# One weight transfer at a time for both tiles of tokens in the feed-forward fronts, h in tiles of 512 by tile of tokens, and parting copies on ScalarE

## The chip, the cores and the metric

The kernel runs on one core of a Trainium2 chip. The metric is the device time of one execution in microseconds (us), median of several runs. A profile is one execution taken by the hardware profiler. Its engines are PE (TensorE, matmul; PEld is its weight load), DVE (VectorE), ACT (ScalarE), POOL (GpSimd), and SP (SyncE, which issues most DMAs).

## The reference, cut to what matters

A decoder trunk of two layers on 256 tokens of width 1024. Each layer is a feed-forward, a mixer and a second feed-forward, each followed by a layer norm:

```python
D_MODEL = 1024; SEQ = 256; DEPTH = 2; D_FF = 2816

def _swiglu(x, w1, w3, w2):
    return (jax.nn.silu(x @ w1) * (x @ w3)) @ w2
...
    for l in range(DEPTH):
        h = _swiglu(x, ffn_w1[l, 0], ffn_w3[l, 0], ffn_w2[l, 0])
        x = _layernorm(ALPHA * x + 0.5 * h, ln_g[l, 0], ln_b[l, 0])
        h = _mixer(...)                       # gated unit, differential attention, merge
        x = _layernorm(ALPHA * x + h, ln_g[l, 1], ln_b[l, 1])
        h = _swiglu(x, ffn_w1[l, 1], ffn_w3[l, 1], ffn_w2[l, 1])
        x = _layernorm(ALPHA * x + 0.5 * h, ln_g[l, 2], ln_b[l, 2])
```

All of it is float32. The change touches the four feed-forwards only.

## The kernel before, in words

**Products in three parts.** Each float32 number is split into a high part (a cast on ACT, `whi`, `hhi`) and the rest (a subtraction on DVE, `wlo`, `hlo`), and each product is three matmuls: high by high, high by low, low by high. Weights come from DRAM through `fetch`, one 1 MB transfer per chunk on SP's queue into one of four `raw` buffers; `stream` splits a chunk into two pieces of 128x1024, by casts and subtractions of width `sub`.

**The front of a feed-forward** (`ffn`) makes h = silu(x W1) * (x W3). Of its 22 column tiles of 128, 20 come in five blocks of 512 columns. Block 0 has a form of its own. Blocks 1 to 4 go through `gemm_b2`: for the first tile of 128 tokens it streams the four chunks of the block (two halves of the contraction `c`, by the two matrices `m`) and multiplies; then it goes over the same pieces again for the second tile of tokens. After each tile, `done` takes the silu of one bank on ACT (L723) and the product with the other on DVE (L724).

**Turning h.** The result has tokens on partitions, and the next matrix needs them on the free axis. So each tile of 128x512 is parted into its 16-bit halves (`parted`, two POOL copies, L199), turned by a DMA transpose that SP issues (`moved`, L203), and joined again (`joined`, POOL copies, L208); then it is split into `h_hi` and `h_lo` in pairs of 128x256 (L743, L745), in tiles that hold both tiles of tokens. These steps are a generator, `turned`, run `beside` the matmuls: it yields how many beats of matmul work to let pass before its next step, 13.3 or 10.3 between parting and transposing.

**The order of work.** TensorE's order is that of the program. On the other engines a scheduler orders by priority, and `behind(ins)` puts an instruction after another one on its engine's queue. The transpose is put behind the newest weight load:

```python
        yield first
        with behind(loaded[0]):
            moved(out, via)
```

**After the front**, two more column tiles come through `gemm_a2`, and `gemm_seven` multiplies by W2: for a square part of the problem by seven products of sums of blocks (L361, each 12 matmuls), each followed by as many ordinary matmuls (L376), then the remaining rows. It fetches two weight blocks into `spare` buffers, which hold x until `gemm_a2` is through with it, adds them on DVE (`plus`, L345), and later adds further blocks to them by accumulating DMAs from POOL's software queue (`gather`, L340):

```python
        product(bx, sums[2], pieces(gather(r2, w22)), False, False)
        ln.fold(1, 1, bx, ALU.subtract, False)
        between()
        product(bx, a22, pieces(gather(r1, w21)), False, True)
```

`fold` (L573, DVE) takes a product out of its bank, which the next product overwrites. Two rows of the norm (`bc`, L540) are loaded by the same software queue in that stage.

Of the kernel before, what the change touches and what calls it, by code (L numbers as in the profile page):

```python
# [54 lines left out]
def trunk(ctx, tc, x, xT, w13a, w13b, w2, wb, wqk, wu, wg, wgr, wbr, wbrr, wo, gateb, gatebr, sgug, sgub, sguwT, sgubias, lam, diffg,  # L55
# [18 lines left out]
    def name(s):  # L74
        serial[0] += 1
        return f"{s}_{serial[0]}"
# [75 lines left out]
    def fetch(src, width=CH, raw=None):  # L152

        step()
        if raw is None:
            raw = raw_pool.tile([P, CH], F32, tag="raw", name=name("raw"))
        for g in gate:
            g[0] -= 1
        while len(gate) > 1 and gate[1][0] < 0:
            gate.pop(0)  # L160
        with behind(gate[0][1] if gate and gate[0][0] < 0 else None):
            loaded[0] = nc.sync.dma_start(raw[:, :width], src).ins
        return raw

    def stream(src, width=CH, sub=HC, lent=(), after=(None, None), pool=()):
# [24 lines left out]
    def planes(v):  # L190
        return v.bitcast(U16).rearrange("p (w c) -> p w c", w=2)

    def numbers(v):
        return v.bitcast(U16).rearrange("p (c w) -> p w c", w=2)

    def parted(src, out):

        for w in range(2):
            G.tensor_copy(out=planes(out)[:, w], in_=numbers(src)[:, w])  # L199

    def moved(src, out):

# [4 lines left out]
        for w in range(2):  # L207
            eng.tensor_copy(out=numbers(out)[:, w], in_=planes(src)[:, w])  # L208

    def transposed(src, out, via, lead, first, second, eng, to=None):  # L210

        if lead:
            yield lead
        with behind(behind_norm[0] if lead else None):
            parted(src, out)
# [85 lines left out]
    def gemm_b(src, kts, xh, xl, done, tail=4, last=()):  # L303
# [13 lines left out]
        for t in range(NT):  # L317
            for ps, o, n in blocks[t]:
                for k, piece in held:
                    rows_b(ps, t, k, piece, xh, xl, kts, o, n)  # L320
                done(t, ps[:, :n], o, n)

    def gemm_seven(src, xh, xl, sums, spare, ln, done):


# [11 lines left out]
        def gather(raw, more):  # L337
            step()
            for o in range(0, CH, HC):
                G.dma_start(raw[:, o : o + HC], more[:, o : o + HC], accum_op=ALU.add)  # L340
            return raw

        def plus(raw, more):
            for o in range(0, CH, HC):
                V.tensor_tensor(out=raw[:, o : o + HC], in0=raw[:, o : o + HC], in1=more[:, o : o + HC], op=ALU.add)  # L345
            return raw

        def pieces(raw):
            out = []
            for o in range(0, CH, HC):  # L350
                hi = hi_pool.tile([P, HC], F32R, tag="hi", name=name("whi"))
                lo = lo_pool.tile([P, HC], F32R, tag="lo", name=name("wlo"))
                split(hi, lo, raw[:, o : o + HC])
                out.append((hi, lo))
            return out

        def product(ps, x, w, start, stop):
            for k in range(4):
                hi, lo = (v[:, k % 2 * 512 : k % 2 * 512 + 512] for v in w[k // 2])
                for n, (y, o) in enumerate(((hi, 0), (lo, 0), (hi, 1))):  # L360
                    PE.matmul(ps, x[o](k), y, start=start and k == n == 0, stop=stop and k == 3 and n == 2,  # L361
                              skip_group_check=True)
                beat(0.25)

        def rest(c):
            for k in range(8, FT, 4):
                nk = min(4, FT - k)
# [3 lines left out]
        def rows(t, c, k0, piece, o=0, n=512):  # L371
            for j in range(2):
                k = k0 + j
                hi, lo = (w[:, j * 512 + o : j * 512 + o + n] for w in piece)
                for m, (y, x) in enumerate(((hi, xh), (lo, xh), (hi, xl))):
                    PE.matmul(q[c][t][:, :n] if o == 0 else more[:, :n], x(k)[:, t * P : (t + 1) * P], y,  # L376
                              start=k == 8 and m == 0 and (c, t) != (1, 0), stop=k == FT - 1 and m == 2, skip_group_check=True)
            beat(n / 1024)

        def block(t, k0):  # L380
            return tuple(lambda k, f=f: f(k0 + k)[:, t * P : (t + 1) * P] for f in (xh, xl))

        a11, a12, a22 = block(0, 0), block(0, 4), block(1, 4)
        first = rest(0)
# [324 lines left out]

    def ffn(l, f, i, norm, last=False):  # L710
        xh, xl = parts(both)
        h_hi = [act.tile([P, 512], F32R, tag="slot", name=name("hhi")) for _ in range(FT // 2)]
        h_lo = [act.tile([P, 512], F32R, tag="slot", name=name("hlo")) for _ in range(FT // 2)]
        hh, hl = view(h_hi), view(h_lo)

        def front(n, wait):

            def done(t, ps):
                pool, tag = ((act, "val"), (res, "bc"))[n % 2]
                p = pool.tile([P, D], F32, tag=tag, name=name("planes"), bufs=2).rearrange("p (w c) -> p w c", w=2)  # L720
                s = p[:, 1]
                with behind(norm.xhi[1, 0] if norm and (n, t) == (0, 0) else None):
                    silu[0] = A.activation(s, ps[0], AF.Silu).ins  # L723
                added[0] = V.tensor_tensor(out=s, in0=s, in1=ps[1], op=ALU.mult).ins  # L724
                beside(turned(n, t, s, p, wait[t]), 0)
                if norm is None and (n, t) == (1, 0):
                    beside(setup(s[:, :1]), 0)
            return done

        def turned(n, t, s, p, wait):  # L730
            lead = 3.5 if n == 0 and norm else 0
            to = slots("held", 2)[0] if n < 2 else p[:, 0]
            yield from transposed(s, p[:, 0], p[:, 1], lead, wait - lead, 0.6, G, to)
            x = to.rearrange("p (k t) -> p k t", k=4)
            yield 0.6
            if n < 2:
                held[n, t] = to
            for j in range(2) if (n, t) != (0, 1) else ():
                k = (n * 4 if n < NB - 1 else FT - 4) // 2 + j
                hi, lo = (v[k].rearrange("p (k t) -> p k t", k=2)[:, :, t * P : (t + 1) * P] for v in (h_hi, h_lo))  # L740
                f = x[:, 2 * j : 2 * j + 2]
                with behind(silu[0]):
                    A.activation(hi, f, AF.Copy)  # L743
                with behind(added[0]):
                    V.tensor_tensor(out=lo, in0=f, in1=hi.bitcast(F32), op=ALU.subtract)  # L745
            if (n, t) == (1, 1):
                yield 1
                yield from sums_of_h()
# [3 lines left out]
        def sums_of_h():  # L752

            h11, h21, h12, h22 = (held[v] for v in ((0, 0), (0, 1), (1, 0), (1, 1)))
            made = [[[v[j].rearrange("p (k t) -> p k t", k=2)[:, :, P:] for j in range(2)] for v in (h_hi, h_lo)]]
            made += [[slots("sum", 2, F32R) for _ in range(2)] for _ in range(2)]
            made.append([[tmp.tile([P, 512], F32R, tag="side", name=name("sum"), bufs=4)] for _ in range(2)])
            sums[:] = [tuple(lambda k, v=v: hh_(v, k) for v in (h_hi, h_lo))]
            sums.extend(tuple(lambda k, v=v: v[0][:, k * P : (k + 1) * P] for v in m) for m in made[1:])
            for n, (out, a, b, op) in ((0, (h22, h21, h22, ALU.subtract)), (2, (h21, h11, h21, ALU.subtract)),  # L760
                                       (1, (h11, h22, h11, ALU.subtract)), (3, (h12, h12, h11, ALU.add))):
                V.tensor_tensor(out=out, in0=a, in1=b, op=op)
                w = 512 // len(made[n][0])
                for j, (hi, lo) in enumerate(zip(*made[n])):
                    f = out[:, j * w : (j + 1) * w]
                    split(hi, lo, f.rearrange("p (k t) -> p k t", k=2) if n == 0 else f)
                yield 1

        def hh_(v, k):
            return v[k // 2][:, k % 2 * T + P : k % 2 * T + T]  # L770

        for n in range(NB):
            srcs = [w13b[l, f, m * NB + n] for m in range(2)]
            if n == 0 and norm is None:
                gemm_first(srcs, front(n, (10.3, 10.3)))
            else:
                gemm_b2(srcs, xh, xl, front(n, (13.3, 10.3)), norm=norm if n == 0 else None)
        for j in range(FA, FT - 4, 2):
            for m, z in gemm_a2([w13a[l, f, j - FA + m] for m in range(2)], both, lambda m: t512("silu")):
                s = z[:, :T]  # L780
                silu[0] = A.activation(s, s, AF.Silu).ins
                V.tensor_tensor(out=s, in0=s, in1=z[:, T:], op=ALU.mult)
                split(hh(j + m), hl(j + m), s)
# [400 lines left out]
```

## Time and profile before

| what | value |
|---|---|
| median of 3 runs | 1199.59 us (1199.42 to 1200.43) |
| the profiled execution | 1198.81 us |
| its span | 1197.1 us |
| granted TensorE clock | 0.999 |
| DMA | 271.97 MB, 227 GB/s in the mean |

The span is the time from the first to the last instruction in the trace; the execution's own time is 1.7 us longer. A row of an engine's timeline has the start, the duration, the line, the operation and its tiles, and in brackets the idle time before it with what ended it. `waits` rows have the engine, what it waited for, and microseconds in total, times and longest. Rows of groups have busy time and mean duration in ns. Rows of windows have start and end, the length, and each engine's busy time with its count of instructions.

### The profile page before, as it was taken

To read this page: it belongs to the slowest core of one execution; us is meant where nothing else is said; L and a number is where in the kernel's file an instruction comes from. 1 tells how busy PE (TensorE), PEld (TensorE's weight loads), DVE (VectorE), ACT (ScalarE), POOL (GpSimd) and SP (SyncE) were. 2 spreads that over 40 slices of the span, in tenths; PEclk is the share of its full clock that TensorE was granted. 3 is DMA by queue.
4 is the path that set the end of the run, shared out by engine and by line. 5 is a ranking of instruction groups with operands and counts; after the bars stand their busy time and mean duration, and the time that the engine had idled before them with its cause. 6 is when DMAs were issued, how large, how long until landed. Compare 5 with 4: busy or idle time off the path is not lost.

```text
span 1197.1 us, 16880 instructions
## 1 busy us (share of the span) xinstructions
PE 1191.1 (100%) x5819; PEld 1002.1 (84%) x5819; DVE 958.4 (80%) x1632; ACT 745.9 (62%) x1424; POOL 363.0 (30%) x458
## 2 busy tenths in 40 slices
PE   9999999999999999999999999999999999999998
PEld 8888888888888888888888888888888888888887
DVE  6677989797689985769886769888966989777795
ACT  7466667668855664646665656666788556564670
POOL 1425201256421233251042351004564012325310
PEclk9999999999999999999999999999999999999999
DMA  9957966767865667689676679586666764775880
GB/s 350 332 163 238 273 263 211 260 198 233 243 218 169 211 220 220 193 245 265 238 241 205 196 241 275 223 287 232 214 203 200 254 193 150 269 230 178 265 253 36
DMA packets 126310, 271.97 MB, mean 227 GB/s; under 512 B 88672, under 2 KB 89744, under 8 KB 100112
## 3 DMA queue, kind: packets, MB, share of 16 engines
q1 hardware_dynamic: 119664, 248.80, 62.4%
q0 software_dynamic: 6128, 21.57, 7.4%
q8 instruction: 45, 0.74, 0.2%
q10 hardware_dynamic: 432, 0.52, 0.1%
q14 instruction: 41, 0.34, 0.1%
HBM read 244.91 MB, written 1.05 MB: 205 GB/s over the span
## 4 chain that ended last, share of the span: by engine, by line
PE 98%; DVE 1%; DMA 1%; ACT 0%; issue 0%; ACTq 0%
PE bank L262 53%; PE bank L274 15%; PE bank L376 9%; PE bank L281 8%; PE sbank L361 5%; PE sbank L376 3%; PE bank L480 2%; PE sbank L843 1%; PE bank L361 1%; PE sbank L899 1%; PE sbank L1017 1%; DMA bc<-in_lng 0%; PE sbank L897 0%; DMA xraw<-in_xT 0%; DVE wlo L186 0%; PE sbank L644 0%
## 5 line engine op out<-in xcount | busy, mean ns | idle before, releaser
L186 DVE TENSOR_TENSOR wlo<-raw,whi 128x512 fp32r<-128x512 f32 (+1 forms) x534 | 473.2, 927 | 52.4 <-ACT whi L184 36.0
L184 ACT ACTIVATE whi<-raw 128x512 fp32r<-128x512 f32 (+1 forms) x538 | 396.1, 782 | 165.7 <-PE bank L262 92.7
L262 PE MATMUL bank<-whi,x 128*128 128x512 f32 x1480 | 460.5, 390 | 0.0
L262 PEld LDWEIGHTS bank<-whi,x 128*128 128x128 f32 x1480 | 277.8, 188 | 57.7
L262 PE MATMUL bank<-wlo,x 128*128 128x512 f32 x740 | 288.0, 389 | 0.0
L199 POOL COPY planes<-planes 128x512 uint16<-128x512 uint16 x80 | 109.6, 1398 | 240.4 <-DVE planes L724 209.4
L262 PEld LDWEIGHTS bank<-wlo,x 128*128 128x128 f32 x740 | 138.9, 188 | 28.3
L274 PE MATMUL bank<-x,whi 128*128 128x512 f32 x640 | 153.3, 391 | 0.0
L274 PEld LDWEIGHTS bank<-x,whi 128*128 128x128 f32 x640 | 118.2, 188 | 23.8
L724 DVE TENSOR_TENSOR planes<-planes,bank 128x512 f32<-128x512 f32 x40 | 27.4, 684 | 75.3 <-issue 60.7
L723 ACT ACTIVATE planes<-bank 128x512 f32<-128x512 f32 x40 | 23.9, 596 | 99.4 <-PE bank L262 97.1
L281 PEld LDWEIGHTS bank<-x,wlo 128*128 128x128 f32 x640 | 81.4, 191 | 2.9
L281 PE MATMUL bank<-x,wlo 128*128 128x256 f32 x640 | 82.6, 283 | 0.0
L228 DVE TENSOR_TENSOR wlo<-raw,whi 128x1024 fp32r<-128x1024 f32 (+1 forms) x56 | 58.5, 1071 | 26.9 <-issue 18.4
L226 ACT ACTIVATE whi<-raw 128x1024 fp32r<-128x1024 f32 (+1 forms) x56 | 52.0, 937 | 42.5 <-DVE raw L345 18.8
L376 PE MATMUL bank<-whi,hhi 128*128 128x512 f32 (+1 forms) x182 | 68.2, 374 | 0.0
L376 PE MATMUL bank<-whi,hlo 128*128 128x512 f32 (+1 forms) x182 | 67.9, 373 | 0.0
L376 PE MATMUL bank<-wlo,hhi 128*128 128x512 f32 (+1 forms) x182 | 67.9, 373 | 0.0
L686 POOL COPY nvia<-ntwo 128x256 uint16<-128x256 uint16 x20 | 9.8, 538 | 155.9 <-DMA ntwo<-nvia 138.3
L819 POOL TENSOR_TENSOR swap<-swap,sin_t 128x512 f32<-128x512 f32 x16 | 26.5, 1655 | 100.8 <-DMA swap<-z 79.5
L282 ACT ACTIVATE r<-bank 128x256 f32<-128x256 f32 x96 | 34.7, 372 | 29.4 <-PE bank L281 29.4
L208 POOL COPY planes<-planes 128x512 uint16<-128x512 uint16 x48 | 36.8, 807 | 17.8 <-DMA planes<-planes 17.4
(246 smaller groups left out, 1857.7 us busy)
## 6 DMA issues: line engine op xcount, KB each, us to landing
raw<-in_w13b SPq DMA_DIRECT2D x76, 1024.0 KB, 5.9
raw<-in_w SPq DMA_DIRECT2D x32, 1024.0 KB, 5.3
raw<-in_wb SPq DMA_DIRECT2D x16, 1024.0 KB, 6.4
raw<-in_wqk SPq DMA_DIRECT2D x16, 1024.0 KB, 6.6
raw<-in_w13a SPq DMA_DIRECT2D x8, 1024.0 KB, 5.2
spare<-in_w SPq DMA_DIRECT2D x8, 1024.0 KB, 5.9
raw<-in_wgr SPq DMA_DIRECT2D x8, 1024.0 KB, 5.4
raw<-in_wg SPq DMA_DIRECT2D x8, 1024.0 KB, 5.1
```

The source lines that it names most:

```text
L184: A.activation(h, r, AF.Copy)
L186: eng.tensor_tensor(out=w, in0=r, in1=h.bitcast(F32), op=ALU.subtract)
L199: G.tensor_copy(out=planes(out)[:, w], in_=numbers(src)[:, w])
L208: eng.tensor_copy(out=numbers(out)[:, w], in_=planes(src)[:, w])
L226: a = A.activation(hi, src, AF.Copy).ins
L228: return a, eng.tensor_tensor(out=lo, in0=src, in1=hi.bitcast(F32), op=ALU.subtract).ins
L262: PE.matmul(ps, xx, w, start=start and n == 0, stop=stop and n == 2)
L274: PE.matmul(b[-1], hi[:, k * P : (k + 1) * P], xc(k), start=k == 0, stop=False)
L281: PE.matmul(b[n][:, :T], lo[:, k * P : (k + 1) * P], xc(k)[:, :T], start=False, stop=k == KT - 1)
L282: emptied[0] = A.activation(r[:, s], b[n][:, T:], AF.Copy, scale=scale).ins
L361: PE.matmul(ps, x[o](k), y, start=start and k == n == 0, stop=stop and k == 3 and n == 2, skip_group_check=True)
L376: PE.matmul(q[c][t][:, :n] if o == 0 else more[:, :n], x(k)[:, t * P : (t + 1) * P], y, start=k == 8 and m == 0 and (c, t) != (1, 0), stop ...
```

## The change

The blocks after the first no longer go through `gemm_b2`. `ffn` loops over the halves `c`, the matrices `m` and the tiles of tokens `t`, so that each streamed chunk is used for both tiles before the next. The silu follows the last chunk of the first matrix and the product that of the second, tile by tile. Pieces are split at the full width of 1024. h lies in tiles of 512 columns by tile of tokens, so that a turned tile is split by one cast and one subtraction. The parting copies of blocks 1 to 4 go to ACT, and the waits before transposing are 9.3 and 8.3. `gather`, `plus`, `pieces` and `product` move out of `gemm_seven` unchanged in what they do; the sums of h are made in the same order, with other pauses. The matmuls stay as many and of the same shapes.

```diff
-    def parted(src, out):
+    def parted(src, out, by=None):
 
         for w in range(2):
-            G.tensor_copy(out=planes(out)[:, w], in_=numbers(src)[:, w])
+            o, i = planes(out)[:, w], numbers(src)[:, w]
+            if by is A:
+                A.activation(o, i, AF.Copy)
+            else:
+                G.tensor_copy(out=o, in_=i)
...
-            for j in range(2) if (n, t) != (0, 1) else ():
-                k = (n * 4 if n < NB - 1 else FT - 4) // 2 + j
-                hi, lo = (v[k].rearrange("p (k t) -> p k t", k=2)[:, :, t * P : (t + 1) * P] for v in (h_hi, h_lo))
-                f = x[:, 2 * j : 2 * j + 2]
-                with behind(silu[0]):
-                    A.activation(hi, f, AF.Copy)
-                with behind(added[0]):
-                    V.tensor_tensor(out=lo, in0=f, in1=hi.bitcast(F32), op=ALU.subtract)
+            if (n, t) != (0, 1):
+                split(h_hi[2 * n + t], h_lo[2 * n + t], to, after=(silu[0], added[0]))
...
-        for n in range(NB):
-            srcs = [w13b[l, f, m * NB + n] for m in range(2)]
-            if n == 0 and norm is None:
-                gemm_first(srcs, front(n, (10.3, 10.3)))
-            else:
-                gemm_b2(srcs, xh, xl, front(n, (13.3, 10.3)), norm=norm if n == 0 else None)
+        if norm is None:
+            gemm_first(w13(0), both_done(0, (10.3, 10.3)))
+        else:
+            gemm_b2(w13(0), xh, xl, both_done(0, (13.3, 10.3)), norm=norm)
+        for n in range(1, NB):
+            ps = [[bank() for _ in range(2)] for _ in range(NT)]
+            ready = front(n, (9.3, 8.3))
+            for c in range(2):
+                for m in range(2):
+                    got = stream(w13(n)[m][:, c * CH : (c + 1) * CH])
+                    for t in range(NT):
+                        for j, piece in enumerate(got):
+                            rows_b(ps[t][m], t, 4 * c + 2 * j, piece, xh, xl, KT)
+                        if c:
+                            ready[m](t, ps[t][m])
```

More of the change, by code (lines that the diff above doesn't have):

```diff
@@ L208, in joined, with transposed @@
             eng.tensor_copy(out=numbers(out)[:, w], in_=planes(src)[:, w])
-    def transposed(src, out, via, lead, first, second, eng, to=None):
+    def transposed(src, out, via, lead, first, second, eng, to=None, by=None):
         if lead:
@@ L216, in transposed @@
         with behind(behind_norm[0] if lead else None):
-            parted(src, out)
+            parted(src, out, by)
         yield first
@@ L321, in gemm_b, with halved, gather, plus @@
                 done(t, ps[:, :n], o, n)
+    def halved(v):
+        return v if isinstance(v, list) else [v[:, o : o + HC] for o in range(0, CH, HC)]
+    def gather(raw, more):
+        step()
+        for j, v in enumerate(halved(raw)):
+            G.dma_start(v, more[:, j * HC : (j + 1) * HC], accum_op=ALU.add)
+        return raw
+    def plus(raw, more):
+        for v, m in zip(halved(raw), halved(more)):
+            V.tensor_tensor(out=v, in0=v, in1=m, op=ALU.add)
+        return raw
+    def pieces(raw):
+        out = []
+        for v in halved(raw):
+            hi = hi_pool.tile([P, HC], F32R, tag="hi", name=name("whi"))
+            lo = lo_pool.tile([P, HC], F32R, tag="lo", name=name("wlo"))
+            split(hi, lo, v)
+            out.append((hi, lo))
+        return out
+    def product(ps, x, w, start, stop):
+        for k in range(4):
+            hi, lo = (v[:, k % 2 * 512 : k % 2 * 512 + 512] for v in w[k // 2])
+            for n, (y, o) in enumerate(((hi, 0), (lo, 0), (hi, 1))):
+                PE.matmul(ps, x[o](k), y, start=start and k == n == 0, stop=stop and k == 3 and n == 2,
+                          skip_group_check=True)
+            beat(0.25)
     def gemm_seven(src, xh, xl, sums, spare, ln, done):
@@ L335, in gemm_seven @@
         (w11, w21), (w12, w22) = ([s[:, o : o + CH] for o in (0, CH)] for s in src)
[L337 to L363, printed above, removed]
         def rest(c):
@@ L711, in ffn, with hv, of @@
         xh, xl = parts(both)
-        h_hi = [act.tile([P, 512], F32R, tag="slot", name=name("hhi")) for _ in range(FT // 2)]
-        h_lo = [act.tile([P, 512], F32R, tag="slot", name=name("hlo")) for _ in range(FT // 2)]
-        hh, hl = view(h_hi), view(h_lo)
+        h_hi, h_lo = ([act.tile([P, 512], F32R, tag="slot", name=name(n)) for _ in range(FT // 2)] for n in ("hhi", "hlo"))
+        def hv(tiles):
+            def of(k, t):
+                if FA <= k < FT - 4:
+                    return tiles[-1][:, (k - FA) * T + t * P : (k - FA) * T + (t + 1) * P]
+                n, k = (k // 4, k % 4) if k < FA else (NB - 1, k - (FT - 4))
+                return tiles[2 * n + t][:, k * P : (k + 1) * P]
+            return of
@@ L716, in front, with gate_, done @@
+        hh, hl = hv(h_hi), hv(h_lo)
         def front(n, wait):
-            def done(t, ps):
+            tiles = {}
+            def gate_(t, ps):
                 pool, tag = ((act, "val"), (res, "bc"))[n % 2]
                 p = pool.tile([P, D], F32, tag=tag, name=name("planes"), bufs=2).rearrange("p (w c) -> p w c", w=2)
+                tiles[t] = p
+                with behind(norm.xhi[1, 0] if norm and (n, t) == (0, 0) else None):
+                    silu[0] = A.activation(p[:, 1], ps, AF.Silu).ins
+            def done(t, ps):
+                p = tiles[t]
@@ L721, in done @@
                 s = p[:, 1]
[L722 to L725, printed above, removed]
+                added[0] = V.tensor_tensor(out=s, in0=s, in1=ps, op=ALU.mult).ins
+                beside(turned(n, t, s, p[:, 0], wait[t]), 0)
                 if norm is None and (n, t) == (1, 0):
@@ L727, in done, with both_done, of @@
                     beside(setup(s[:, :1]), 0)
-            return done
+            return gate_, done
+        def both_done(n, wait):
+            gate_, done = front(n, wait)
+            def of(t, ps):
+                gate_(t, ps[0])
+                done(t, ps[1])
+            return of
         def turned(n, t, s, p, wait):
             lead = 3.5 if n == 0 and norm else 0
-            to = slots("held", 2)[0] if n < 2 else p[:, 0]
-            yield from transposed(s, p[:, 0], p[:, 1], lead, wait - lead, 0.6, G, to)
@@ L734, in turned @@
-            x = to.rearrange("p (k t) -> p k t", k=4)
+            to = slots("held", 2)[0] if n < 2 else p
+            yield from transposed(s, p, s, lead, wait - lead, 0.6, G, to, A if n else G)
             yield 0.6
@@ L760, in sums_of_h @@
-            for n, (out, a, b, op) in ((0, (h22, h21, h22, ALU.subtract)), (2, (h21, h11, h21, ALU.subtract)),
-                                       (1, (h11, h22, h11, ALU.subtract)), (3, (h12, h12, h11, ALU.add))):
+            made = [[h_hi[1], h_lo[1]]] + [[slots("sum", 2, F32R)[0] for _ in range(2)] for _ in range(2)]
+            made.append([tmp.tile([P, 512], F32R, tag="side", name=name("sum"), bufs=4) for _ in range(2)])
+            yield from strassen_sums(sums, made, h11, h21, h12, h22)
@@ L767, in sums_of_h, with w13 @@
                 yield 1
[L769 to L777 removed]
+        def w13(n):
+            return [w13b[l, f, m * NB + n] for m in range(2)]
```

29 lines of the change are left out of this document (16 added, 13 removed).

## The prediction

> **What bounds the kernel now.** I read the page's busy times first, then TensorE's waits, then the chain of waits, and last the stages in which that chain has no slack.
>
> ```profile
> PE 1191.1 (100%) x5819; PEld 1002.1 (84%) x5819; DVE 958.4 (80%) x1632; ACT 745.9 (62%) x1424; POOL 363.0 (30%) x458
> ```
>
> TensorE works for 1191.1 of 1197.1 us. Its waits are short:
>
> ```profile
> PE sbank L492 <- DVE warm L488: 1.1, 1, 1.1
> PE sbank L623 <- ACT minus L621: 0.7, 1, 0.7
> ```
>
> The two longest sum to 1.8 us, and the change touches neither. The number of matmuls and their shapes stay the same. So the change can save next to nothing: whatever it does for the other engines is hidden, and the question is only whether something comes late for TensorE. Of a difference, about 0.2% (2.4 us) can be told from none in this kernel.
>
> **The fronts (blocks 1 to 4 of each feed-forward).** The chain of waits shows the four blocks of one front as one piece, and the windows show what lies beside it:
>
> ```profile
> 27.19 87.04 PE bank L262 x384
> ```
>
> ```profile
> 27.00:114.00 87.00, 87.00 (x385) 72.04 (x384) 64.67 (x108) 51.20 (x92) 36.93 (x42) 1.00 0.80 250
> ```
>
> The columns of a window are its sum, then PE, PEld, DVE, ACT and POOL busy with their instructions, clock, DMA share, GB/s. 87.04 us for 384 matmuls is 0.2267 us each with no hole; a block is 8 steps of 12 matmuls, a step 2.72 us. In these 87 us DVE is busy 74%, ACT 59%, POOL 42%, DMA 80%.
>
> What the change does here, from the rows that group the operations by shape:
>
> ```profile
> L184 ACT ACTIVATE whi<-raw 128x1024 fp32r<-128x1024 f32 x200 | 205.2, 1053 | 67.6 <-PE bank L274 30.8 <-PE bank L262 29.1 <-DMA raw<-in_w 5.7
> L184 ACT ACTIVATE whi<-raw 128x512 fp32r<-128x512 f32 x338 | 190.9, 622 | 98.2 <-PE bank L262 63.6 <-PE bank L376 18.0 <-PE bank L274 5.1
> L199 POOL COPY planes<-planes 128x512 uint16<-128x512 uint16 x80 | 109.6, 1398 | 240.4 <-DVE planes L724 209.4 <-ACT whi L184 30.9
> L637 ACT ACTIVATE nvia<-xtok 128x512 uint16<-128x512 uint16 x10 | 6.3, 628 | 3.1 <-DVE xtok L598 3.1
> L724 DVE TENSOR_TENSOR planes<-planes,bank 128x512 f32<-128x512 f32 x40 | 27.4, 684 | 75.3 <-issue 60.7
> ```
>
> Casts: 256 of 622 ns become 128 of 1053 ns, 24 us less on ACT. Parting copies: 64 leave POOL (at 1398 ns, 89 us less) and come to ACT at about 628 ns (the ACT copy of that shape), 40 us more. ACT gains 16 us net, over the four fronts: 62% becomes 63 to 64%. DVE loses 128 instructions (1587 to 1459). None of it is on the path. The order of the work moves more: both tiles now finish in the last half of a block, with the silus after steps 5 and 6 and the products after steps 7 and 8. In the built order the bank of the last product is written again three steps (8.16 us) after the block, and that product takes 0.68 us; so some 7 us are left. The weight pieces are held for two steps instead of being read twice, half a block apart, so their buffers come free evenly, a chunk every 5.44 us. I cost the fronts at zero. If the cover were gone, the price would be a fraction of a step, 1 us a block, but I see no row near that. Below nothing isn't possible either, since TensorE has no hole there to close.
>
> **What is moved.** The last block's two DMA transposes are the catch. Each is ordered behind the newest weight load at its time. Before, the two products of that block came half a block apart, and the waits before its transposes put them ahead of the load that is issued at 120.20:
>
> ```profile
> 111.70 7.97 SPq L203 DMA_TRANSPOSE planes<-planes  x2
> 120.20 0.34 SPq L162 DMA_DIRECT2D raw<-in_w  x1
> 124.87 0.81 SPq L162 DMA_DIRECT2D spare<-in_w  x2
> 127.63 27.58 SPq L162 DMA_DIRECT2D raw<-in_w  x5
> ```
>
> Afterwards, by the built order of the SyncE queue, in all four feed-forwards, they stand behind that load and behind both `spare` loads, ahead of the next. So they move from 111.70 and 118.44 to about 126, past three loads of 1 MB. The `spare` loads themselves wait for TensorE to free a buffer at 124.87 and can't come earlier. The windows show what this means for the DMA engines (the DMA share is the last column but one):
>
> ```profile
> 117.00:122.00 5.00, 5.00 (x26) 4.24 (x25) 0.94 (x1) 1.21 (x2) 3.53 (x5) 1.00 0.44 85
> 122.00:127.00 5.00, 5.00 (x37) 4.67 (x35) 4.47 (x10) 3.64 (x11) 0.72 (x2) 1.00 0.67 234
> 127.00:132.00 5.00, 5.00 (x24) 4.14 (x23) 5.00 (x11) 2.29 (x6) 1.43 (x3) 1.00 0.99 412
> 132.00:142.00 10.00, 10.00 (x46) 8.29 (x45) 10.00 (x11) 6.78 (x8) 2.05 (x3) 1.00 1.04 266
> 142.00:152.00 10.00, 10.00 (x46) 8.29 (x45) 9.46 (x11) 6.02 (x7) 1.14 (x2) 1.00 1.02 264
> ```
>
> One transpose lay where the engines were 0.44 busy. They now go into a stretch that is full (0.99 to 1.04) until 152. What one costs, from the DMA answer for 119 to 121 us, in which only that transpose ran:
>
> ```profile
> q1 hardware_dynamic: 1056, 0.26, 58.1%
> ```
>
> 58.1% of 2 us is 1.16 us of all 16 engines for 0.26 MB, in 1056 small packets. Two make 2.3 us of backlog, in each feed-forward.
>
> **Who waits for the end of that stretch.** Last in it come the accumulating gathers of the seven-product stage (`gather`, the software queue); the second half of the last one feeds the seventh product (L361, at 157.99). ACT, then DVE, then the chain of waits:
>
> ```profile
> 151.40 1.06 ACT L226 ACTIVATE whi<-raw 128x1024 fp32r<-128x1024 f32 x1 [1.60 <-DMA raw<-in_w]
> 152.50 1.23 DVE L228 TENSOR_TENSOR wlo<-raw,whi 128x1024 fp32r<-128x1024 f32 x1 [1.03 <-ACT whi L226]
> 153.64 3.49 DVE L186 TENSOR_TENSOR wlo<-raw,whi 128x1024 fp32r<-128x1024 f32 x3
> 157.04 0.68 DVE L573 SCALAR_TENSOR_TENSOR xtok<-xtok,sbank 128x512 f32<-128x512 f32 x1
> 157.99 2.89 PE sbank L361 x12
> ```
>
> ACT idles 1.60 us for the gather, DVE idles 1.03 us for ACT, then three more subtractions and the fold (L573) that empties the bank which the seventh product writes. The fold ends at 157.72, and the product, 2.89 us instead of 2.72, has already been held for 0.17 us. Nothing is spare here: what the gather slips, TensorE waits. In the built order the same subtractions stand before that fold. In the second, third and fourth feed-forward:
>
> ```profile
> 571.18 0.68 DVE L573 SCALAR_TENSOR_TENSOR xtok<-xtok,sbank 128x512 f32<-128x512 f32 x1
> 572.24 0.39 PE L361 MATMUL sbank<-whi,hhi 128*128 128x512 f32 x1
> 748.95 0.68 DVE L573 SCALAR_TENSOR_TENSOR xtok<-xtok,sbank 128x512 f32<-128x512 f32 x1
> 749.82 0.44 PE L361 MATMUL sbank<-whi,hhi 128*128 128x512 f32 x1
> 1157.17 1.06 ACT L226 ACTIVATE whi<-raw 128x1024 fp32r<-128x1024 f32 x1 [1.39 <-DMA raw<-in_w]
> 1157.76 2.36 DVE L228 TENSOR_TENSOR wlo<-raw,whi 128x1024 fp32r<-128x1024 f32 x2
> 1163.43 0.69 DVE L573 SCALAR_TENSOR_TENSOR xtok<-xtok,sbank 128x512 f32<-128x512 f32 x1
> 1164.60 0.39 PE L361 MATMUL sbank<-whi,hhi 128*128 128x512 f32 x1
> ```
>
> The second has 572.24 - 571.86 = 0.4 us to spare, the third 0.2 at most (I take 0.1, its first matmul is drawn out). The fourth has 1164.60 - 1164.12 = 0.5 at the fold, and its second subtraction (1158.94, half of 2.36 us in) starts 0.7 us after the cast ended at 1158.23: 1.2 together. Their DMA is as full:
>
> ```profile
> 545.00:567.00 22.00, 22.00 (x98) 18.21 (x98) 21.24 (x23) 14.35 (x15) 3.52 (x4) 1.00 1.00 274
> 723.00:745.00 22.00, 22.00 (x99) 18.22 (x98) 21.06 (x23) 14.59 (x15) 3.47 (x4) 1.00 1.00 267
> 1137.00:1159.00 22.00, 21.85 (x97) 17.76 (x96) 21.20 (x25) 16.29 (x18) 4.11 (x5) 1.00 1.00 264
> ```
>
> **The sum.** How far the last gather slips isn't in the trace. Low end 0: the backlog falls on loads that have time. High end 4.6 us: the gather's delayed tail takes turns with the next weight load, so that 2.3 us of work need twice as long. I take 2.0, near the 2.3 that a full DMA hands on one for one, less a little for the weight load that is issued beside the gathers and takes part of it. Stalls: 2.0 + (2.0 - 0.4) + (2.0 - 0.1) + (2.0 - 1.2) = 6.3 us. The profiled execution took 1198.81 us (span 1197.1, and 1.7 around it): 1198.81 + 6.3 = 1205.1. The median of the runs is 0.8 above the profiled one, so 1205.9 us. By the high end it is 4.6 + 4.2 + 4.5 + 3.4 = 16.7, about 1216; by the low end 1199.6.
>
> The moved transposes also put POOL's joining copies and two casts of h later on their engines, behind the first gathers and among the casts of the fourth product:
>
> ```profile
> 141.67 2.72 PE sbank L361 x12
> ```
>
> Its second half starts 1.36 us in, at 143.0. A transpose that is issued at about 128 (after the two `spare` issues, which end at 125.7, and the first transpose) and lands 4.4 to 8.1 us later, by two rows below, leaves 7 us or more for two copies and a cast. I cost that at nothing.
>
> **Rivals.** *No change* (1199.6 us, chance 0.26). The place is the same stretch, from 132 to 151 us. If the gathers go first and the backlog falls on the weight loads of the first hardware queue, whose next reader on ACT stands behind the gather's own cast, the last gather lands as before. It holds as long as the slips beyond the slack sum to under 2.4 us, 0.9 us a gather or less (0.9 + 0.5 + 0.8 + 0 = 2.2). For it: ACT and DVE lose some h work ahead of the stage, and the gather may be issued a little earlier. Against it: DMA shares of 1.00 to 1.04 in four stages, which leave no hole to absorb 2.3 us.
>
> *The transposes land too late* (about 1219 us, chance 0.06). If they must wait among the gathers until the middle of the last full window, 147, the cast that stands behind h's casts ends at 148.05 at the earliest (1.05 us a cast), and the fourth product's second half, due at 143.0, waits 5 us, 20 in all: 1199.6 + 20 = 1219.6. It decides from a landing at about 142. Two transposes elsewhere bear on it, the first with no transfers of the software queue beside it, the second with four:
>
> ```profile
> on<-onT SPq DMA_TRANSPOSE x1, 4.4
> on<-onT SPq DMA_TRANSPOSE x1, 8.1
> ```
>
> A transpose takes 3.7 us longer in such company. At 8.1 from 128 it lands at 136.1, 6 us before it would hurt, so I give this little. The Trainium skill ("DMA: Bandwidth & Descriptors", section "Queues, rings and completion order") has each DMA engine switch between queues only after a whole packet of one. By that rule, read strictly, hundreds of tiny transpose packets a queue could each be held up by one large gather packet, and this rival would come true, at 1219 us; the 8.1 us speaks against so strong an effect.
>
> *Faster* (chance 0.03): TensorE's idle time of 6 us lies mostly at the two ends, so over 2.4 us of gain has no place to come from.
>
> **How the numbers follow.** The forecast, a slip of about 2 us at the seventh product, has 0.65; with the late transposes 0.06, slower has 0.71, same 0.26, faster 0.03. The likeliest case's own range is 1202.0 to 1214. The range for 8 in 10 takes in most of the no-change case and most of the high end: 1199.3 to 1213.5.
>
> **What would show it.** In the profile after: TensorE's pieces before the seventh products (157.99, 572.24, 749.82, 1164.60) begin later by 2.0, 1.6, 1.9 and 0.8, with the fold late and behind it a cast that waits for DMA; the fronts are still one piece of 87.04 us; the transposes start after the `spare` loads and the DMA share stays at 1.0 past 152. I am wrong if the last gather lands within 0.5 us of its old distance from the stage's start, if the lost time lies in the fronts, or if the fourth product waits.

## The result, and the profile after

The changed kernel takes 1250.5 to 1254.4 us, against 1199.84 for the one before: the ratio is 1.0441 (1.0419 to 1.0463), and in a second series 1.0468 (1.0421 to 1.0515). It is slower by about 54 us, where 6 were forecast. One run, the profiled one, lay at 2011 us with the clock at 0.556 throughout; the lines below are of another profile of the same kernel (span 1248.9 us).

Busy times and TensorE's waits, to be held against those of before:

```profile
PE 1209.0 (97%) x5819; PEld 1010.3 (81%) x5819; DVE 949.0 (76%) x1464; ACT 766.5 (61%) x1320; POOL 309.2 (25%) x394
```

```profile
PE sbank L358 <- ACT whi L234: 26.7, 7, 6.7
PE sbank L358 <- DVE wlo L236: 4.5, 8, 0.7
PE sbank L358 <- DVE xtok L584: 2.7, 1, 2.7
```

The span grew by 51.8 us. TensorE idles 39.9 us in place of 6.0, 33.9 more, which are the three waits (26.7 + 4.5 + 2.7), all at products of the seven-product stage (L358 now). The same matmuls take 17.9 us longer. Both happen in that stage of each feed-forward; by feed-forward the three waits sum to 9.4, 6.9, 7.9 and 9.8 us. The windows of the first (the last three columns are the granted clock, the DMA share and GB/s):

```profile
27.00:114.00 87.00, 87.00 (x386) 72.03 (x385) 60.01 (x74) 55.07 (x71) 35.20 (x28) 1.00 0.80 258
...
132.00:137.00 5.00, 5.00 (x24) 4.14 (x23) 4.95 (x5) 3.50 (x4) 1.76 (x2) 1.00 1.27 110
137.00:142.00 5.00, 4.79 (x22) 3.62 (x20) 2.48 (x3) 0.00 (x0) 0.00 (x0) 1.00 1.15 170
142.00:147.00 5.00, 0.00 (x0) 0.00 (x0) 0.00 (x0) 0.19 (x1) 1.42 (x2) 0.71 1.08 179
147.00:152.00 5.00, 2.84 (x6) 1.79 (x6) 2.42 (x3) 1.39 (x2) 1.12 (x2) 0.50 1.14 309
152.00:157.00 5.00, 3.02 (x7) 1.78 (x6) 3.05 (x4) 4.66 (x6) 1.95 (x3) 0.50 0.77 157
157.00:162.00 5.00, 5.00 (x22) 4.04 (x22) 5.00 (x6) 3.67 (x4) 0.00 (x0) 0.92 0.74 132
```

The front is as full as before. From 141.8 TensorE stands still for 6.65 us, and after one matmul for 0.7 more; then it works at half its clock, with a pause, until past 157. The chain of waits names the cause:

```profile
27.32 87.04 PE bank L270 x384
...
125.89 19.42 DMA planes<-planes
145.36 1.43 POOL planes L216 x2
146.81 0.64 ACT hhi L234
149.95 2.52 PE sbank L358 x5
```

The first of the two moved transposes is issued at 125.89 and lands 19.42 us later. POOL's joining copies follow, and ACT's cast of h. On ACT that cast stands ahead of a weight cast of the fourth product:

```profile
146.81 0.63 ACT L234 ACTIVATE hhi<-planes 128x512 fp32r<-128x512 f32 x1 [11.23 <-POOL planes L216]
147.35 1.04 ACT L234 ACTIVATE whi<-raw 128x1024 fp32r<-128x1024 f32 x1
152.34 0.63 ACT L234 ACTIVATE hhi<-planes 128x512 fp32r<-128x512 f32 x1 [3.95 <-POOL planes L216]
152.88 1.04 ACT L234 ACTIVATE whi<-raw 128x1024 fp32r<-128x1024 f32 x1
```

ACT idles 11.23 us at the head of its queue for a piece of h that TensorE needs only later, and the weights behind it come late. Their own data was there long before: DVE had ended the sums that the two weight casts read at 139.5.

```profile
137.13 2.35 DVE L342 TENSOR_TENSOR raw<-raw,spare 128x1024 f32<-128x1024 f32 x2
```

The second transpose holds the product's second half in the same way. The POOL timeline of the other feed-forwards has the same long waits:

```profile
571.27 1.41 POOL L216 COPY planes<-planes 128x512 uint16<-128x512 uint16 x2 [10.22 <-DMA planes<-planes]
759.79 1.42 POOL L216 COPY planes<-planes 128x512 uint16<-128x512 uint16 x2 [9.64 <-DMA planes<-planes]
1188.37 3.04 POOL L216 COPY planes<-planes 128x512 uint16<-128x512 uint16 x2 [10.68 <-DMA planes<-planes]
```

The second and third feed-forward stall as the first does. The last has the late landing too, but its stall starts one product earlier and by another piece of work. ACT scales a row of the norm (L570) ahead of a weight cast of the third product, and the row's load by the software queue, issued at 1172.13, is late as well. Later in the same stage the seventh product waits for the fold (ACT, then TensorE):

```profile
1185.88 1.06 ACT L570 ACTIVATE bc<-bc 128x1024 f32<-128x1024 f32 x1 [9.44 <-DMA bc<-in_lng]
1186.84 1.04 ACT L234 ACTIVATE whi<-raw 128x1024 fp32r<-128x1024 f32 x1
1187.93 0.79 PE L358 MATMUL sbank<-whi,hhi 128*128 128x512 f32 x1 [6.19 <-ACT whi L234]
1214.70 0.47 PE L358 MATMUL sbank<-whi,hhi 128*128 128x512 f32 x1 [2.68 <-DVE xtok L584]
```

The granted clock of 0.50 after 6.65 us of idle time agrees with the Trainium skill ("TensorE: Matmul & The Clock Gate", section "Part 1: The HAM clock gate"): the page has the array's clock halved after an idle window of some 3.4 us, and released after as long a busy one. Here it stayed at half longer than that, from 147 to 157. The product ran in two bursts with idle time between, the first from 149.95 to 152.47, shorter than such a window; that would explain it, but no run tests it. In the run with filled idle time below, 2.77 us without a matmul were enough for the clock to fall, less than the page's window; there the measurement decides.

### The profile page after: what moved, and what is told of

It is laid out like the page before. It is cut to its first block, busy times and chain, and to the rows that moved or that the text cites. A ratio compares the mean times of both kernels' runs of the same rounds, so it can differ in the third digit from the quotient of the medians.

```text
span 2009.8 us, 16591 instructions
## 1 busy us (share of the span) xinstructions
PE 2001.5 (100%) x5819; PEld 1226.6 (61%) x5819; DVE 952.9 (47%) x1464; ACT 783.2 (39%) x1320; POOL 253.7 (13%) x394
## 4 chain that ended last, share of the span: by engine, by line
PE 98%; DMA 1%; issue 0%; POOL 0%; ACT 0%; DVE 0%; SPq 0%; ACTq 0%; POOLq 0%
PE bank L270 53%; PE bank L282 15%; PE bank L387 9%; PE bank L289 7%; PE sbank L358 5%; PE sbank L387 3%; PE bank L491 2%; DMA planes<-planes 1%; PE sbank L880 1%; PE bank L358 1%; PE sbank L936 1%; PE sbank L1054 1%; PE sbank L934 0%; PE sbank L655 0%; DMA xraw<-in_xT 0%
## 5 line engine op out<-in xcount | busy, mean ns | idle before, releaser
L270 PE MATMUL bank<-whi,x 128*128 128x512 f32 x1480 | 716.6, 577 | 0.0
L190 DVE TENSOR_TENSOR wlo<-raw,whi 128x1024 fp32r<-128x1024 f32 (+1 forms) x406 | 461.2, 1152 | 502.0 <-ACT whi L188 453.8
L188 ACT ACTIVATE whi<-raw 128x1024 fp32r<-128x1024 f32 (+1 forms) x410 | 392.1, 970 | 698.0 <-PE bank L270 356.7
L270 PEld LDWEIGHTS bank<-whi,x 128*128 128x128 f32 x1480 | 323.6, 219 | 242.3 <-issue 141.6
L270 PE MATMUL bank<-wlo,x 128*128 128x512 f32 x740 | 426.2, 576 | 0.0
L282 PE MATMUL bank<-x,whi 128*128 128x512 f32 x640 | 254.0, 576 | 0.0
L289 PEld LDWEIGHTS bank<-x,wlo 128*128 128x128 f32 x640 | 126.3, 260 | 13.0 <-issue 8.5
L289 PE MATMUL bank<-x,wlo 128*128 128x256 f32 x640 | 130.1, 383 | 0.0
L236 DVE TENSOR_TENSOR wlo<-raw,whi 128x1024 fp32r<-128x1024 f32 (+1 forms) x56 | 59.5, 1086 | 85.6 <-ACT whi L234 46.5
L216 POOL COPY planes<-planes 128x512 uint16<-128x512 uint16 x48 | 42.6, 933 | 314.7 <-DMA planes<-planes 302.9
L234 ACT ACTIVATE whi<-raw 128x1024 fp32r<-128x1024 f32 (+1 forms) x56 | 51.7, 932 | 54.9 <-DVE raw L342 19.9
L270 PE MATMUL bank<-lhi,x 128*128 128x512 f32 x120 | 59.5, 575 | 0.0
L387 PEld LDWEIGHTS bank<-whi,hhi 128*128 128x128 f32 x182 | 41.9, 230 | 25.0 <-issue 14.2
```

Of the source, the lines that this page charges most:

```text
L188: A.activation(h, r, AF.Copy)
L190: eng.tensor_tensor(out=w, in0=r, in1=h.bitcast(F32), op=ALU.subtract)
L234: a = A.activation(hi, src, AF.Copy).ins
L236: return a, eng.tensor_tensor(out=lo, in0=src, in1=hi.bitcast(F32), op=ALU.subtract).ins
L270: PE.matmul(ps, xx, w, start=start and n == 0, stop=stop and n == 2)
L282: PE.matmul(b[-1], hi[:, k * P : (k + 1) * P], xc(k), start=k == 0, stop=False)
```

## The experiments

**The change once more** (the profile shown above).

> The changed kernel once more, for a profile at full clock. Theory A (turns): the two transposes of the last block, now behind the spare loads, take turns packet by packet with the software queue's transfers, land some 15 to 20 us after their issue, and hold the fourth and the following products; then four places in the trace, one per feed-forward, hold nearly all of the 50 us, some 12 us each, part of it idle time of TensorE and part a lower granted clock after it; the fronts stay one piece of 87.04 us. Theory B (backlog): each place costs about 2 us at the seventh product, and over 40 us are lost in the fronts. Theory C (clock): the new order of the fronts' matmuls lowers the granted clock evenly, about 0.98 in every stage, and no stall over 3 us is seen.

Measured: 1254.49 us. Theory A has the place and the landing (19.4 us), and the fourth product in three feed-forwards of four; in the last it is the third product, behind the scaling of the norm's row. Its 12 us per feed-forward are in the mean 33.9 / 4 = 8.5 of idle time and 17.9 / 4 = 4.5 of low clock.

**The transposes ahead of the spare loads.**

```diff
-            ready = front(n, (9.3, 8.3))
+            ready = front(n, (9.3, 8.3) if n < NB - 1 else (7.3, 6.3))
```

> The changed kernel with shorter waits for the last block alone (7.3 and 6.3 in place of 9.3 and 8.3), which puts its two transposes ahead of the load before the spare loads, where they stood before the change. Theory A: 1199 to 1202 us, all of the loss gone, the transposes land within 5 us. Theory B: 1240 to 1246, only the 2 us per feed-forward come back. Theory C: 1250, no change.

Measured: 1204.03 us, ratio 1.0033 (1.0021 to 1.0044). Of 54 us, 50 are gone with an edit of two waits in one block. 4 us are left, which theory A did not have; they are taken up below.

**Only the place, in the kernel before.** This is the converse: nothing of the change but the place of the two transposes.

```diff
-                gemm_b2(srcs, xh, xl, front(n, (13.3, 10.3)), norm=norm if n == 0 else None)
+                gemm_b2(srcs, xh, xl, front(n, (13.3, 10.3) if n < NB - 1 else (12.3, 8.3)), norm=norm if n == 0 else None)
```

> The kernel before with one thing changed: for the last block, the waits before the two transposes are 12.3 and 8.3 in place of 13.3 and 10.3. The transposes are so written down one to two beats earlier, when the newest load is still the second spare load, and stand behind both spare loads on SP, as in the change. No other part of the change is in it. Theory A (transposes that take turns with the software queue's transfers): about as slow as the change, 1235 to 1260 us, with stalls of some 10 us at the fourth product of each feed-forward and the granted clock down to 0.5 behind each. Theory D (it needs the rest of the change too, such as pieces and casts in another order): 1200 to 1215.

Measured: 1239.85 us, ratio 1.0347 (1.0316 to 1.0377). The place alone costs 40 us, with TensorE's busy time at 1204.5 us and 0.50 of the clock from 147 to 157. Three feed-forwards have one stall of 5.7 to 10.7 us each. The last has 3.1 us, again behind the scaling of the norm's row (L559 here), which waited 6.34 us for its load.

**Plain copies in their place.** The last block's pieces of h stay unturned in this kernel.

```diff
-    def moved(src, out):
-
+    def moved(src, out, plain=False):
+        if plain:
+            return nc.sync.dma_start(out.bitcast(U16), src.bitcast(U16)).ins
         return nc.sync.dma_start(out.bitcast(U16).rearrange("p (k t) -> p k t", t=P), src.bitcast(U16),
                                  transpose=True).ins
```

> The changed kernel with the last block's two transposes replaced, at the same place in the queue, by plain copies of the same bytes (128 rows of 2 KB each in place of many packets of 256 bytes), so that h of that block is not turned. Theory A: the copies have a handful of packets per engine and land within 10 us of their issue; the loss goes nearly whole, 1200 to 1206 us. If what matters is only the place behind the spare loads, whatever the packets: 1235 to 1255. Theory C: 1250.

Measured: 1208.18 us, ratio 1.0069 (1.0054 to 1.0084). The same bytes at the same place in 2 KB rows, by the median of their DMA answer:

```profile
planes<-planes SPq DMA_DIRECT2D x2, 256.0 KB, 10.2
```

They land after 10.2 us, behind the 2 MB of the spare loads, so the place costs a part too; the 46 us that went belong to the transposes' kind of transfer. What stays are waits of TensorE for DVE, 1.6 to 2.2 us per feed-forward. The timelines of DVE and POOL show the joining copies now beside DVE's sums:

```profile
137.77 3.37 DVE L343 TENSOR_TENSOR raw<-raw,spare 128x1024 f32<-128x1024 f32 x2
...
135.75 6.01 POOL L217 COPY planes<-planes 128x512 uint16<-128x512 uint16 x4 [1.87 <-DMA planes<-planes]
```

Two of these sums took 2.36 us before. The Trainium skill ("SBUF — State Buffer", section "SBUF: two separate sides") has VectorE and GpSimd share a port pair that one of them locks for a whole instruction, and the 1.0 us that the two sums lose beside the copies agrees. TensorE's longest wait is 1.7 us there, and its clock stays at 1.00.

**One of the two late.**

```diff
+            ready = front(n, (9.3, 8.3) if n < NB - 1 else (7.3, 8.3))
```

> The changed kernel with the first of the last block's two transposes put ahead (7.3 in place of 9.3) and the second left behind the spare loads. Theory A: the one that is left has half as many small packets to take turns with, lands some 10 us after its issue, and costs from 0 to 5 us per feed-forward, 1200 to 1220 us. Theory B: 1 us per feed-forward less than the change, 1246. Theory C: 1250.

Measured: 1212.2 us, ratio 1.0111 (1.0087 to 1.0134). In the first feed-forward the late one lands 10.0 us after its issue, in place of 19 and 22. Two late transposes cost more than four times what one costs. In three feed-forwards the late one nearly meets the fourth product's due time (waits of 0.5 to 0.7 us). In the last TensorE waits 4.7 us, but at the third product: ACT's scaling of the norm's row stands ahead of its cast and waits for the row's load.

```profile
1149.45 1.06 ACT L570 ACTIVATE bc<-bc 128x1024 f32<-128x1024 f32 x1 [8.11 <-DMA bc<-in_lng]
```

**Without the gathers**, so that of the software queue only the norm's rows (1 MB) run beside the transposes.

```diff
-        for j, v in enumerate(halved(raw)):
-            G.dma_start(v, more[:, j * HC : (j + 1) * HC], accum_op=ALU.add)
```

> The changed kernel without the accumulating gathers (4 transfers of 512 KB per feed-forward left out, so that two weight sums are incomplete). The transposes stay behind the spare loads; the norm's two rows still go by the software queue. Theory A: with 1 MB in place of 3 MB to take turns with, the transposes land within 10 us of their issue; stalls shrink to 0 to 3 us per feed-forward, 1198 to 1212 us. If the transposes were slow by themselves behind the spare loads: 1240 and more.

Measured: 1231.89 us, ratio 1.0263 (1.0243 to 1.0283). My number was wrong: the transposes still land 14.2 us after their issue. 1 MB is enough. The first window of the contention moves 113 GB/s at a share of 1.07 (windows of this kernel), where the kernel before, gathers included, moved 291 at 1.01:

```profile
132.00:137.00 5.00, 5.00 (x24) 4.14 (x23) 4.95 (x6) 3.35 (x4) 0.00 (x0) 1.00 1.07 113
```

So "taking turns" in the sense of my first theory is too mild. While both kinds are there, the engines count as busy and move little.

**Nothing of the software queue beside them**, and then **the gathers alone**. In both the norms' rows go by SP's queue; the first leaves the gathers out, the second has them.

```diff
-        spread[0] = G.dma_start(t, src.partition_broadcast(P)).ins
+        spread[0] = (nc.sync if src.shape[-1] == D and t_sync[0] else G).dma_start(t, src.partition_broadcast(P)).ins
```

`t_sync` is set around the two loads of a norm's rows, so that no other load changes its queue.

> The changed kernel without the gathers (left out as before) and with the norms' rows loaded by SP's queue in place of the software queue, so that nothing of the software queue runs beside the late transposes; their place behind the spare loads stays (the two rows stand between the spare loads). Theory A (contention with the software queue): each transpose lands some 3 us after the transfers ahead of it, at about 135 and 137 us in the first feed-forward, in place of 145 and 151; 1199 to 1206 us. If the place alone makes them slow: they land after 141, and 1225 or more.

> The same with the gathers kept, so that they alone run beside the late transposes. Theory A: the gathers start later than the norm's rows did, at about 134 us, so a part of the transposes' packets is through before; they land between 137 and 145 us and the loss is between nothing and half of the change's: 1203 to 1228 us. If only the norm's rows (broadcast reads) disturb the transposes: 1199 to 1203.

Measured: 1206.19 us, ratio 1.0052 (1.0037 to 1.0067), and 1276.97 us, ratio 1.0658 (1.0603 to 1.0713). The landings of the two transposes of the first feed-forward, before, in the change, in the first and in the second of these, from the DMA answers about their issue:

```profile
planes<-planes SPq DMA_TRANSPOSE x2, 4.4
```

```profile
planes<-planes SPq DMA_TRANSPOSE x2, 20.5
```

```profile
planes<-planes SPq DMA_TRANSPOSE x2, 7.9
```

```profile
planes<-planes SPq DMA_TRANSPOSE x2, 27.2
```

This pair settles it: same place, same packets, and 71 us between them by the gathers alone. With nothing of the software queue there, the kernel is 6 us slower than the one before, so the place behind the spare loads costs no more than that. With the gathers by themselves it is worse than the change, not milder as I had expected; the window shows how little moves:

```profile
137.00:142.00 5.00, 4.71 (x21) 3.57 (x19) 1.76 (x2) 0.42 (x1) 0.00 (x0) 1.00 1.17 45
```

The DMA engines count as fully busy at 45 GB/s.

**Filling the idle time**, to separate the stall from the clock.

```diff
-        product(bx, sums[1], pieces(plus(r1, r3)), False, False)
+        w4, fill = pieces(plus(r1, r3)), bank()
+        for j in range(28):
+            PE.matmul(fill, a11[0](j % 4), pieces1[0][0][:, :512], start=True, stop=True)
+        product(bx, sums[1], w4, False, False)
```

> The changed kernel with 28 matmuls of 128x512 (6.3 us at the full clock, into a bank that nobody reads) put on TensorE ahead of each fourth product, where it idles some 8 us. If the idle time itself brings the lower clock afterwards, the clock stays at 1.0 and 12 to 18 us of the loss come back: 1235 to 1243 us. If the clock falls for another reason, or the stall is only moved: 1254 or more.

Measured: 1259.5 us, ratio 1.0501 (1.0479 to 1.0522). Inconclusive. In this run the first transpose lands 21.88 us after its issue, later than in the change, so a gap is left behind the filling, and the clock falls all the same:

```profile
141.54 6.51 PE L415 MATMUL bank<-whi,hhi 128*128 128x512 f32 x28
150.82 0.79 PE L358 MATMUL sbank<-whi,sum 128*128 128x512 f32 x1 [2.77 <-ACT whi L234]
```

It shows that 2.77 us of idle time are enough here (the next matmul takes 0.79 us in place of 0.39, and the granted clock is 0.50 from 152 to 157), while the 1.7 us with plain copies were not. Whether a filling without a gap keeps the clock was not seen.

**What was left: 4 us.** With the transposes ahead, the waits that remain are nearly all in the last feed-forward, where ACT scales a row of the norm (L570) as soon as it is loaded, ahead of the casts for the third product (ACT's timeline of the kernel with the shorter waits):

```profile
1142.36 1.06 ACT L570 ACTIVATE bc<-bc 128x1024 f32<-128x1024 f32 x1 [5.12 <-issue]
1143.33 1.99 ACT L234 ACTIVATE whi<-raw 128x1024 fp32r<-128x1024 f32 x2
```

The casts' data was there at 1140.3 (DVE's sums ended). In the kernel before, the scheduler had them first (1137.34, the scaling at 1141.03). Two runs separate this from the choice of waits, both with waits of 10.3 and 9.3 for the last block, the second also with

```diff
-                A.activation(self.g, self.g, AF.Copy, scale=-0.5)
...
+            if self.last and (t, c) == (0, 0):
+                with behind(cast[0]):
+                    A.activation(self.g, self.g, AF.Copy, scale=-0.5)
```

> The changed kernel with only the waits of the last block one beat longer (10.3 and 9.3), which puts the transposes ahead of the spare loads; the scaling of the norm's row stays where the change has it. If that scaling, which holds the third product's casts on ACT in the last feed-forward, cost the 3 to 4 us that were left with the transposes ahead, this run takes 1203 to 1204.5 us; if the choice of the waits did, 1199.5 to 1201.

> The changed kernel with waits of 10.3 and 9.3 for the last block, one beat later than in the change, so that the newest load is again the one before the spare loads and the transposes stand ahead of them; and with the scaling of the norm's row in the last feed-forward (an ACT cast that waits for its load and stood ahead of the third product's casts) put behind the casts. Theory A: 1199.5 to 1201 us, the same as the kernel before, since TensorE has no hole to give. If anything else in the change costs time: 1202 to 1205, as with the transposes ahead by a shorter wait (1204.0).

Measured: 1203.98 us, ratio 1.0033 (1.0020 to 1.0046), and 1200.06 us, ratio 1.0001 (0.9992 to 1.0010). So the change has two costs and no third: with both mended it runs as the kernel before, no faster. The mended kernel's front in the chain of waits:

```profile
28.10 87.04 PE bank L270 x384
```

And the scaling mended with the transposes left late:

> The changed kernel with its own waits (transposes behind the spare loads) and with the scaling of the norm's row put behind the casts. If the two costs add up, 1249 to 1252 us, 3 to 4 less than the change; if the scaling hides in the stall of the last feed-forward, the same as the change, 1253 to 1255; if it is a part of why the change loses 14 us more than the kernel before with late transposes, 1240 to 1246.

Measured: 1261.74 us, ratio 1.0515 (1.0499 to 1.0531). None of the three cases: it is 7 us slower. TensorE's waits tell where. In the last feed-forward they sum to 9.4 us, against 9.8 in the change: with the scaling out of the way, h's cast holds the fourth product there as in the others, so each of the two delays hides the other. The 7 us lie in the first and third (12.6 us each, against 9.4 and 7.9), which the edit of the scaling does not touch. Under this contention the landing shifts from kernel to kernel (the first transpose lands after 23.6 us in the first feed-forward here, after 19.4 in the change), so single microseconds of it can't be added or taken away. It stays open why the kernel before with late transposes loses 40 us and the change 54.

## Why the prediction was wrong

*What bounds it, and the fronts.* Right. TensorE's piece of the front is 87.04 us before, after and in the mended kernel, and the parting copies, the wider casts and the new loop cost nothing (1200.06 against 1200.04). One count was off without harm: DVE has 168 instructions fewer (1632 to 1464 on the pages), not 128, since the wider split of h saves some too.

*What is moved.* Right: the two transposes stand behind the spare loads, and that is where the time goes. The reason I gave was half of it. Each is ordered behind the newest load when it is written down. Before, they were written one and two beats after an ordinary weight load, and so stood behind a load that goes early, ahead of the one issued at 120.20. In the change they are written one to two beats sooner, when the newest load is the second spare load, which goes late. Sooner in the program became later on the queue; a wait longer by one beat mends it.

*What a transpose costs.* Here it failed. I took 1.16 us of the engines, measured where a transpose ran alone, and added 2.3 us of backlog to the last gather. The step "lands 4.4 to 8.1 us later ... leaves 7 us or more", which I "cost at nothing", was the wrong one: it landed after 19.4. I had taken the 8.1 us beside four transfers for a bound, but that was one transpose beside four transfers of 256 KB; here two stood beside four of 512 KB. The rival "the transposes land too late", to which I gave 0.06, is what happened, in three feed-forwards by the very path described (late landing, h's cast at the head of ACT's queue, the fourth product). Its landing was close (147 assumed, 145.3 measured), and its 5 us per feed-forward were sized too low: the stalls there are 9.4, 6.9 and 7.9, since the second transpose holds the second half once more, and the low clock after them, which I had not counted, is 4.5 in the mean. In the last feed-forward the 9.8 us come nearly all by two paths that the rival did not have: the software queue's own load of the norm's row was late, and then the gather.

*The rule.* I set the arbitration of the queues as the Trainium skill has it ("DMA: Bandwidth & Descriptors", section "Queues, rings and completion order") against the 8.1 us and let the row win. The runs side with the rule in its direction: with the software queue away the transposes land after 7.9 us, with the gathers after 27.2. That turns between whole packets are the cause was not shown; why the engines moved so little meanwhile, the rule as cited does not say.

*The seventh product.* The stall that I forecast there is seen in the last feed-forward alone, where it is 2.68 us by the path forecast (gather, cast, fold) against 0.8 forecast. That gather was issued late, at 1197.48, behind POOL's joining copies of the late pieces of h. In the other three TensorE does not wait there; in the first it came to that product 13 us late. Whether 2.3 us of backlog would have reached it can't be told from these runs.

*The scaling in the last feed-forward* was in the built order and I did not see it: 4 us with early transposes, and with late ones the 6.19 us stall of the third product.

## What to carry to other kernels

When a change leaves the bound engine full, look for what it moves on the queues rather than for what it removes, and check for each moved transfer what kind of traffic runs at its new place, not only how full the engines are. A price measured alone, or beside other transfers, is no bound for a transfer of many tiny packets beside a software queue. And a piece of work that is not urgent should not stand at the head of an in-order queue ahead of work that is: a cast needed much later turned a late transfer into a stall of the whole core.

## What the runs showed of the hardware

A DMA transpose of 0.26 MB, some 1050 packets, takes 1.16 us of the engines alone and lands after 2.7 to 4.4 us at the early place (the kernel before and the mended one). Two of them beside transfers of the software queue landed after some 13 to 28 us, a single one after 8.1 and 10.0. In the slowest window of 5 us both kinds together moved 110 GB/s in the change, 113 with the norm's rows alone and 45 with the gathers alone, at a DMA share over 1.0. Why the engines are busy with so little was not settled. One stall of 2.77 us was followed by 0.50 of TensorE's clock; one of 1.7 us was not.
